# The low half of the feed-forward weights: a negated copy on ScalarE and an adding transfer instead of a VectorE subtraction

## The chip, the core and the metric

The kernel runs on one core of a Trainium2 chip, alone. The metric is the time of one execution on the device in microseconds (us), as the median of its runs. The engines are named as in the profile: PE is TensorE (matmul), PEld its weight load, DVE is VectorE, ACT is ScalarE, POOL is GpSimd, SP is SyncE. SPq, ACTq and POOLq stand for the instruction queues of those engines when they only issue transfers or wait.

## The reference, cut to what matters

One inference step of a two-layer decoder on 512 prompt tokens and 8 sample tokens, model width 1024. Layer one mixes tokens with sliding-window attention, layer two with gated linear attention (GLA). Each is followed by the same gated feed-forward block, and each sublayer by a LayerNorm. The change touches only the weights of the feed-forward block:

```python
D_MODEL = 1024; D_FF = 2816; CONV_W = 3; DEPTH = 2

def conv_ffn(x, buf, w_up, conv_w, conv_b, w_down):
    T = x.shape[1]
    h = x @ w_up                              # (T, 2 * D_FF)
    a, u = h[..., :D_FF], h[..., D_FF:]       # gate, value
    ap = jnp.concatenate([buf.astype(a.dtype), a], axis=1)
    c = conv_b + sum(conv_w[j] * ap[:, j:j + T] for j in range(CONV_W))
    y = (jax.nn.gelu(c, approximate=False) * u) @ w_down
    return y, ap[:, T:]

for i in range(DEPTH):
    ...
    xp = layer_norm(ALPHA * xp + mp, ln_mix_g[i], ln_mix_b[i])
    fp, cp = conv_ffn(xp, buf0, ffn_w_up[i], ffn_conv_w[i], ffn_conv_b[i], ffn_w_down[i])
    xp = layer_norm(ALPHA * xp + fp, ln_ffn_g[i], ln_ffn_b[i])
```

All data are float32.

## The kernel before, in words

**Products in two parts.** The matmuls run in float32r, a shorter format. Each operand is split into a high part (the value rounded to float32r) and a low part (the value minus its high part, also stored as float32r). A product is the sum of three matmuls: high weight by high activation, high weight by low activation, low weight by high activation. In the profile the tiles of the weights are `raw` (the float32 weights as loaded), `wh` (high) and `wl` (low).

**Units.** All weights are cut into 187 units of 128 output features. A unit is a tile of 128 partitions by 1024 elements (512 KB); the first part of a down-projection has units of 128 by 768 (384 KB). Units 0 to 9 are the attention projections, 10 to 17 its output projection, 18 to 85 the feed-forward block of layer one, 86 to 110 GLA, 111 to 118 its output projection, 119 to 186 the feed-forward block of layer two. A feed-forward block has 44 units of the up-projection (gate and value in turn, `ffn_gate` and `ffn_value`) and 24 of the down-projection (`ffn_down`), in three parts: after 6, 14 and 22 pairs of gate and value comes a run of eight down units.

**Two groups of tokens.** Each unit is used twice: by group a (256 prompt tokens) and later by group b (256 prompt tokens and the 8 samples). `order` (line 996 on) writes the PE order of the blocks: block (a, u) is followed by block (b, u minus the lead). The lead is `max(LAG, min(top, p0 + 2 * top - u))`: 5 for the first units of a phase, 4 from the seventh unit on. So in the middle of a feed-forward block the order is (a, u), (b, u - 4), (a, u + 1), (b, u - 3) and so on.

**Buffers of the weights.** `raw` has 2 buffers. `wh` and `wl` have 6 slots, and during a feed-forward block one more (`wx`, the extra slot). A slot is free when group b has used its unit. `run` calls `next_unit` after each b block, and that issues the next load; with seven slots the unit loaded after (b, u) is u + 7. The extra slot is not refilled in the last eight units before the end of each feed-forward block; after that the unit loaded after (b, u) is u + 6. This holds for the last six units of each block, 80 to 85 and 181 to 186.

**Loading a unit** (`load_unit`, line 152 on). SP issues the transfer from DRAM into `raw` (line 162). ACT writes `wh`, a rounding copy (line 167). DVE writes `wl = raw - wh` (line 170). For the few units loaded around the start of a feed-forward block or of GLA (flag `late`) the two steps are traced by `parts` instead (ACT line 181, DVE line 183). Of the 136 feed-forward units 12 are late ones (19 to 24 and 120 to 125).

**Use of a unit.** In most feed-forward blocks group a uses `product2`: for each of the 8 slices of the contraction, one matmul with the high weights over 512 columns (high and low activations side by side, line 221) and one with the low weights over 256 columns (line 222). The low weights are read from the second matmul of the block on. Group b uses `product`: three matmuls for each slice (lines 198, 200 and 202), the third with the low weights. The first four pairs of gate and value and the third part of the down-projection use `product` for group a too.

**What else runs in the feed-forward block.** ACT copies the gate's sums out of PSUM (line 637), scales (642), applies GELU (653) and rounds the product gate times value (228). DVE does the convolution's multiply-adds (643, 644), the product (665) and its low part (229). POOL clears or copies the two columns of history (634, and the copies on line 232). PSUM holds four accumulators.

**Order on each engine.** The kernel is written with the Tile framework, opened with `schedule_with_timeline_sim=True`: the framework takes the instructions in the order in which the program traces them as priorities, and places each on its engine's queue when its own simulation has it ready. So an edit can also change the order of instructions around it. Each engine runs its queue in order.

Of the kernel before, what the change touches and what calls it, by code (L numbers as in the profile page):

```python
# [11 lines left out]
F32 = mybir.dt.float32  # L12
F32R = mybir.dt.float32r
I32 = mybir.dt.int32
AF = mybir.ActivationFunctionType
ALU = mybir.AluOpType
# [81 lines left out]
class Net:  # L98
# [53 lines left out]
    def load_unit(self, u, pieces=1, extra=False, late=False):  # L152
        src, nt = self.units[u][0], self.units[u][1]
        nc = self.nc
        if nt == 0:
            return self.load_rank(u)
        r = self.raw.tile([P, KD * P], F32, name="raw")
        pool = self.wx if extra else self.wts
        h, l = (pool.tile([P, KD * P], F32R, name=name) for name in ("wh", "wl"))
        n = nt * P // pieces  # L160
        for c in (slice(i * n, (i + 1) * n) for i in range(pieces)):
            nc.sync.dma_start(out=r[:, c], in_=src[:, c])
            if late:
                self.spawn(self.parts(u, h[:, c], l[:, c], r[:, c]), 1)
                continue
            if u >= HIACT:
                nc.scalar.activation(h[:, c], r[:, c], AF.Copy)  # L167
            else:
                nc.gpsimd.tensor_scalar(h[:, c], r[:, c], 1.0, 0.0, op0=ALU.mult, op1=ALU.add)
            nc.vector.tensor_tensor(l[:, c], r[:, c], h[:, c].bitcast(F32), op=ALU.subtract)  # L170
        self.w[u] = (h, l)

# [1000 lines left out]
```

## Time and profile before

| | |
|---|---|
| median of 2 runs | 1133.96 us (1133.62 to 1134.3) |
| span of the profiled execution, first to last instruction | 1131.7 us |
| PE busy | 1104.2 us, 98% |
| DVE, ACT, POOL busy | 777.2 us (69%), 565.7 us (50%), 319.3 us (28%) |
| moved by the transfers | 122.81 MB, 109 GB/s over the span |
| feed-forward block of layer one, about | 160 to 520 us of the span |
| feed-forward block of layer two, about | 770 to 1107 us of the span |

The profiled execution is one execution taken by the hardware profiler; of its own time only the span is known, 2.3 us less than the median of the runs. The page's parts are: busy time of each engine, the span in 40 slices, the transfer queues, the chain of work that ended last, groups of instructions, and transfers. A row of a group names line, engine, operation, the tile written and the tiles read, partitions by elements, the count, the busy time, the mean duration in ns, and the idle time of the engine just before, with what ended it. In a timeline each row is: start, duration, engine, line, operation, tiles, and in brackets the idle time before it and what released it. Matmuls overlap: the next starts before the last one's shown end, so the step from start to start is what a matmul costs.

### The profile page before, as it was taken

What the parts mean: (1) busy time and instruction counts of PE and PEld (TensorE: products, weight loads), DVE (VectorE), ACT (ScalarE), POOL (GpSimd) and SP (SyncE); (2) the same over time, 40 slices, a digit from 0 to 9 for tenths busy, and PEclk for the clock granted to TensorE, in tenths of its full rate; (3) what the DMA queues carried; (4) which work ended last, traced back from release to release, by engine and by line L of the source; (5) the groups of instructions that cost most, each with busy time, mean ns of one, the idle gap of its engine ahead of it and who ended that gap; (6) DMA issues with size and microseconds to landing.
All of it is one profiled execution on the core that took longest, in us unless ns stands there. A gap on an engine that the chain in (4) does not pass through costs nothing.

```text
span 1131.7 us, 22912 instructions
## 1 busy us (share of the span) xinstructions
PE 1104.2 (98%) x8806; PEld 1055.1 (93%) x8806; DVE 777.2 (69%) x1626; ACT 565.7 (50%) x1251; POOL 319.3 (28%) x591
## 2 busy tenths in 40 slices
PE   8999999999999999999999999999999999999996
PEld 7997799999999999999899999899999999999995
DVE  7897579655665566568867778779756665566565
ACT  5677556534553245435455556456524553245433
POOL 4575574400110011255211100374400110001243
PEclk9999999999999999999899999999999999999998
DMA  7553023333233233242124354432333223223222
GB/s 244 150 178 96 16 75 101 105 103 121 94 105 102 93 100 106 75 134 94 57 90 145 122 178 160 139 111 94 113 98 127 94 98 109 93 96 110 76 64 76
DMA packets 53804, 122.81 MB, mean 109 GB/s; under 512 B 6808, under 2 KB 27328, under 8 KB 53696
## 3 DMA queue, kind: packets, MB, share of 16 engines
q1 hardware_dynamic: 51536, 119.47, 32.8%
q10 hardware_dynamic: 2160, 1.89, 0.5%
q8 instruction: 69, 1.13, 0.4%
q14 instruction: 39, 0.32, 0.1%
HBM read 108.67 MB, written 8.47 MB: 104 GB/s over the span
## 4 chain that ended last, share of the span: by engine, by line
PE 77%; DVE 10%; DMA 5%; ACT 3%; issue 2%; POOL 1%; SPq 0%; ACTq 0%; DVEq 0%; POOLq 0%
PE accp L198 16%; PE accp L200 16%; PE accp L202 16%; PE accp L221 15%; PE accp L222 8%; DMA vb<-dv 2%; DVE xs_a L355 1%; DVE wl L183 1%; DVE wl L170 1%; DMA raw<-in_w_up 1%; DMA qs<-hl 1%; DVE sgla L910 1%; DVE x_a L353 1%; PE pv L554 1%; ACT pr L523 1%
## 5 line engine op out<-in xcount | busy, mean ns | idle before, releaser
L170 DVE TENSOR_TENSOR wl<-raw,wh 128x1024 fp32r<-128x1024 f32 (+2 forms) x172 | 207.0, 1205 | 103.3 <-ACT wh L167 102.7
L198 PE MATMUL accp<-xh_b,wh 128*128 128x264 f32 x976 | 272.5, 279 | 1.8 <-ACT xh_b L354 1.7
L167 ACT ACTIVATE wh<-raw 128x1024 fp32r<-128x1024 f32 (+2 forms) x168 | 173.6, 1033 | 199.8 <-PE accp L200 187.3
L202 PE MATMUL accp<-xh_b,wl 128*128 128x264 f32 x976 | 270.8, 277 | 0.0
L200 PE MATMUL accp<-xl_b,wh 128*128 128x264 f32 x960 | 266.5, 278 | 0.0
L221 PE MATMUL accp<-xs_a,wh 128*128 128x512 f32 x576 | 196.3, 382 | 0.0
L198 PEld LDWEIGHTS accp<-xh_b,wh 128*128 128x128 f32 x976 | 184.8, 189 | 3.3 <-ACT xh_b L354 2.3
L202 PEld LDWEIGHTS accp<-xh_b,wl 128*128 128x128 f32 x976 | 184.5, 189 | 0.8 <-issue 0.6
L200 PEld LDWEIGHTS accp<-xl_b,wh 128*128 128x128 f32 x960 | 181.6, 189 | 2.5 <-issue 0.4
L222 PE MATMUL accp<-xs_a,wl 128*128 128x256 f32 x576 | 145.4, 273 | 0.0
L198 PE MATMUL accp<-hh_b,wh 128*128 128x264 f32 x480 | 134.2, 280 | 1.7 <-ACT hh_b L228 1.1
L200 PE MATMUL accp<-hl_b,wh 128*128 128x264 f32 x480 | 134.6, 280 | 0.3 <-DVE hl_b L594 0.2
L202 PE MATMUL accp<-hh_b,wl 128*128 128x264 f32 x480 | 133.6, 278 | 0.0
L221 PEld LDWEIGHTS accp<-xs_a,wh 128*128 128x128 f32 x576 | 109.1, 189 | 11.4
L222 PEld LDWEIGHTS accp<-xs_a,wl 128*128 128x128 f32 x576 | 110.2, 191 | 1.9
L198 PE MATMUL accp<-xs_a,wh 128*128 128x256 f32 x400 | 107.6, 284 | 1.4 <-ACT wh L167 0.6
L200 PE MATMUL accp<-xs_a,wh 128*128 128x256 f32 x384 | 103.0, 282 | 0.6 <-DVE xs_a L229 0.3
L198 PEld LDWEIGHTS accp<-hh_b,wh 128*128 128x128 f32 x480 | 91.6, 191 | 2.3 <-ACT hh_b L228 1.6
L200 PEld LDWEIGHTS accp<-hl_b,wh 128*128 128x128 f32 x480 | 91.5, 191 | 1.8 <-DVE hl_b L594 0.4
L202 PEld LDWEIGHTS accp<-hh_b,wl 128*128 128x128 f32 x480 | 91.5, 191 | 0.2
L232 POOL COPY hist<-aext 128x2 f32<-128x2 f32 x44 | 10.2, 231 | 283.7 <-DVE aext L641 277.2
L198 PEld LDWEIGHTS accp<-xs_a,wh 128*128 128x128 f32 x400 | 77.2, 194 | 2.8 <-ACT wh L167 1.0
(338 smaller groups left out, 2505.5 us busy)
## 6 DMA issues: line engine op xcount, KB each, us to landing
raw<-in_w_up SPq DMA_DIRECT2D x88, 512.0 KB, 3.4
raw<-in_w_down SPq DMA_DIRECT2D x32, 512.0 KB, 3.4
raw<-in_w_gla SPq DMA_DIRECT2D x24, 512.0 KB, 3.4
raw<-in_w_mix_o SPq DMA_DIRECT2D x16, 512.0 KB, 4.1
raw<-in_w_down SPq DMA_DIRECT2D x16, 384.0 KB, 3.0
qs<-hl SPq DMA_DIRECT2D x64, 64.0 KB, 2.2
sgla<-in_state_gla SPq DMA_DIRECT2D x16, 256.0 KB, 2.7
vb<-dv SPq DMA_DIRECT2D x16, 256.0 KB, 3.7
```

What stands on the lines that cost most here:

```text
L167: nc.scalar.activation(h[:, c], r[:, c], AF.Copy)
L170: nc.vector.tensor_tensor(l[:, c], r[:, c], h[:, c].bitcast(F32), op=ALU.subtract)
L183: self.nc.vector.tensor_tensor(l, r, h.bitcast(F32), op=ALU.subtract)
L198: nc.tensor.matmul(o, h[:, ks], xh, start=k == 0, stop=False)
L200: nc.tensor.matmul(o, h[:, ks], xl, start=False, stop=False)
L202: nc.tensor.matmul(o, l[:, ks], xh, start=False, stop=not tail and k == nt - 1)
L221: both = lambda: nc.tensor.matmul(o, h[:, ks], in_turn(rs[:, k].rearrange("p t q j -> p t (q j)")), start=k == 0, stop=last)
L222: low = lambda: nc.tensor.matmul(o[:, :P], l[:, ks], in_turn(rh[:, k]), start=False, stop=False)
L353: v = nc.vector.scalar_tensor_tensor(x[:, m], x[:, m], sc(m), rp, op0=ALU.mult, op1=ALU.mult)
L355: xl = nc.vector.scalar_tensor_tensor(g.xl[:, m], parted(x[:, m]), bi(m), g.xh[:, m].bitcast(F32), op0=ALU.add, op1=ALU.subtract)
L523: nc.scalar.activation(pr[:, b, 0:P + 1], sc[:, b, 0:P + 1], AF.Exp, bias=nm[:, b:b + 1], accum_out=den[:, b:b + 1])
L554: mm = nc.tensor.matmul(pv[64 * v:64 * v + 64, b * P:(b + 1) * P], self.vtok[:, kb, 64 * v:64 * v + 64], parts[v][w][:, b], start=i == 0, ...
```

## The change

For feed-forward units that are not late ones, DVE's subtraction is taken out. In its place ACT reads `wh` again and writes its negative into `wl`, and POOL issues a transfer that adds float32 weights onto `wl` where it lies in SBUF. In layer one (`first`: the unit's first argument is the layer) the transfer reads the weights a second time from DRAM. In layer two it reads them from `raw` in SBUF.

```diff
             if u >= HIACT:
                 nc.scalar.activation(h[:, c], r[:, c], AF.Copy)
             else:
                 nc.gpsimd.tensor_scalar(h[:, c], r[:, c], 1.0, 0.0, op0=ALU.mult, op1=ALU.add)
+            if self.units[u][2] in (self.ffn_gate, self.ffn_value, self.ffn_down):
+                first = self.units[u][3][0] == 0
+                nc.scalar.activation(l[:, c], h[:, c].bitcast(F32), AF.Copy, scale=-1.0)
+                nc.gpsimd.dma_start(out=l[:, c], in_=src[:, c] if first else r[:, c], accum_op=ALU.add)
+                continue
             nc.vector.tensor_tensor(l[:, c], r[:, c], h[:, c].bitcast(F32), op=ALU.subtract)
         self.w[u] = (h, l)
```

The `late` branch stands above these lines and ends with its own `continue`, so the late units keep DVE's subtraction, as do the units of attention, GLA and the output projections. The first unit of each feed-forward block (18 and 119) is loaded in the phase before and takes the new lines.

## The prediction

> **What bounds the kernel now.** I read the page first, then the stages, PE's waits, and a timeline from the middle of layer one's feed-forward block.
>
> ```profile
> span 1131.7 us, 22912 instructions
> ...
> PE 1104.2 (98%) x8806; PEld 1055.1 (93%) x8806; DVE 777.2 (69%) x1626; ACT 565.7 (50%) x1251; POOL 319.3 (28%) x591
> ...
> q1 hardware_dynamic: 51536, 119.47, 32.8%
> ...
> raw<-in_w_up SPq DMA_DIRECT2D x88, 512.0 KB, 3.4
> ```
>
> Two stages, one inside each feed-forward block (columns: stage, its length, busy time and instructions of PE, PEld, DVE, ACT, POOL, granted clock, transfer share, GB/s), and the stage at the end:
>
> ```profile
> 300.00:500.00 200.00, 200.00 (x1550) 193.27 (x1549) 119.36 (x220) 88.09 (x160) 29.28 (x83) 1.00 0.31 104
> 786.00:930.00 144.00, 144.00 (x1100) 138.72 (x1099) 93.11 (x175) 68.98 (x128) 24.65 (x71) 1.00 0.33 107
> ...
> 1100.00:1132.00 32.00, 21.25 (x174) 20.38 (x173) 18.38 (x39) 12.59 (x27) 12.77 (x19) 0.88 0.20 67
> ```
>
> What PE waits for that the change touches (total us, times, longest):
>
> ```profile
> PE accp L198 <- ACT wh L167: 0.6, 2, 0.5
> ...
> PE accp L202 <- DVE wl L170: 0.6, 1, 0.6
> ```
>
> PE is the bound: in the feed-forward blocks it never idles, and its idle time in the whole span is 1131.7 - 1104.2 = 27.5 us, a good part of it at the end. DVE's subtraction costs PE 0.6 us in all. So taking it away can gain next to nothing; the question is whether the new, longer way to `wl` stays hidden behind PE.
>
> **The cover there is today.** The timeline, cut to the rows that time one slot:
>
> ```profile
> 404.18 0.28 PE L202 MATMUL accp<-hh_b,wl 128*128 128x264 f32 x1
> 404.43 1.06 ACT L167 ACTIVATE wh<-raw 128x1024 fp32r<-128x1024 f32 x1 [0.83 <-PE accp L200]
> 405.52 1.23 DVE L170 TENSOR_TENSOR wl<-raw,wh 128x1024 fp32r<-128x1024 f32 x1 [0.60 <-ACT wh L167]
> 406.78 0.33 SPq L162 DMA_DIRECT2D raw<-in_w_up  x1
> 409.70 1.06 ACT L167 ACTIVATE wh<-raw 128x1024 fp32r<-128x1024 f32 x1 [1.05 <-PE accp L200]
> 409.83 0.27 PE L222 MATMUL accp<-xs_a,wl 128*128 128x256 f32 x1
> 415.02 1.06 ACT L167 ACTIVATE wh<-raw 128x1024 fp32r<-128x1024 f32 x1 [0.68 <-PE accp L200]
> 415.15 0.27 PE L222 MATMUL accp<-xs_a,wl 128*128 128x256 f32 x1
> ```
>
> At 404.18 group b's block (b, u) ends. That frees a slot, and ACT, which had waited for it, starts the copy for unit u + 7 at 404.43. The period of one unit is 415.15 - 409.83 = 5.32 us. With seven slots and a lead of 4 the PE order after (b, u) is (a, u + 5), (b, u + 1), (a, u + 6), (b, u + 2), (a, u + 7). So the new slot's low part is first read two periods on, at 415.15: 10.72 us after ACT's start. Today it is written at 405.52 + 1.23 = 406.75, which leaves 8.4 us of slack.
>
> The same rows show a second ring. SP's load at 406.78 follows the end of the subtraction by 0.03 us: `raw` has two buffers, and it is the subtraction that frees one.
>
> The last six units of each block have one slot fewer. In layer two they show as ACT's copies after a period without one:
>
> ```profile
> 1057.63 1.06 ACT L167 ACTIVATE wh<-raw 128x1024 fp32r<-128x1024 f32 x1 [1.05 <-PE accp L200]
> 1068.33 1.06 ACT L167 ACTIVATE wh<-raw 128x1024 fp32r<-128x1024 f32 x1 [4.29 <-PE accp L200]
> ...
> 1096.11 1.07 ACT L167 ACTIVATE wh<-raw 128x1024 fp32r<-128x1024 f32 x1 [0.26 <-PE accp L200]
> ```
>
> For those the time to the first low matmul is one period less: 10.72 - 5.32 = 5.4 us.
>
> **The change part by part.** Of 136 feed-forward units 12 are late ones and stay, so 124 change, 62 in each layer, 8 of each 62 with 768 columns.
>
> ```profile
> L170 DVE TENSOR_TENSOR wl<-raw,wh 128x1024 fp32r<-128x1024 f32 x150 | 187.7, 1252 | 90.0 <-ACT wh L167 89.5 <-PE accp L202 0.3
> L170 DVE TENSOR_TENSOR wl<-raw,wh 128x768 fp32r<-128x768 f32 x16 | 15.3, 958 | 13.2 <-ACT wh L167 13.2
> ...
> L167 ACT ACTIVATE wh<-raw 128x1024 fp32r<-128x1024 f32 x150 | 158.8, 1059 | 169.2 <-PE accp L200 157.1 <-DMA raw<-in_w_mix_o 7.5 <-DMA raw<-in_w_up 1.5
> L167 ACT ACTIVATE wh<-raw 128x768 fp32r<-128x768 f32 x16 | 13.5, 846 | 30.1 <-PE accp L200 30.1
> ```
>
> *Removed.* DVE: 108 x 1.252 + 16 x 0.958 = 151 us. By PE's waits worth 0.6 us at most; I take 0.
>
> *ACT, the negation.* The same size as the copy before it: 108 x 1.06 + 16 x 0.85 = 128 us. Per unit ACT goes from 68.98 / 144 x 5.32 = 2.5 to 3.6 us of 5.32, so it fits. Behind it stand the copies that empty PSUM, at most 1.06 us later; four accumulators cover that (two blocks are 5.32 us). Cost 0 beside its part in the chain below. Without that cover each block would lose up to 1 us.
>
> *POOL, the issue.* POOL is busy 24.65 of 144 us here. Behind the issue in its queue stand the tiny history copies:
>
> ```profile
> L232 POOL COPY nconv_p<-aext 128x2 f32<-128x2 f32 x44 | 29.9, 679 | 118.3 <-ACT aext L637 118.2
> L232 POOL COPY hist<-aext 128x2 f32<-128x2 f32 x44 | 10.2, 231 | 283.7 <-DVE aext L641 277.2 <-ACT aext L637 6.6
> ```
>
> They feed the next convolution, not PE, and have idle time ahead of them: cost 0. If the issue is queued behind such a copy instead, it waits for DVE, some 1.5 us; that belongs to the range.
>
> *The adding transfer.* No transfer on POOL's queue and no adding one is in this trace. Let X be the time from the end of the negation until `wl` is readable. The nearest row is the plain 512 KB load, from issue to landing (least, median, most):
>
> ```profile
> DMA to landing us min/median/max: 2.8/3.4/5.9
> ```
>
> Lower bound: a plain load, 3.4 us. Upper bound: two of the slowest ones in sequence, as the transfer reads two operands, 11.8 us. In between: a load's share of the 16 transfer engines is 0.328 x 1131.7 / 119.47 x 0.524 = 1.63 us. A second read costs between that and a whole load, so about 2.5 us. POOL's issue I estimate at 1.0 us against SP's 0.33 (its copy of two columns already takes 0.68), so 0.7 more. X = 3.4 + 2.5 + 0.7 = 6.6 us, nearer to the lower bound since the pieces of one transfer overlap.
>
> The Trainium skill, Collectives: The Full Stack, section "The bandwidth ceiling: the fold count and why AG ≠ RS ≠ AR", says that adding in a transfer costs through its two source reads, both on one ring, and not through the addition. By that the second read would be 1.63 us, X 5.7 and the sum below about 1168. No run here shows it yet.
>
> *The chain.* From ACT's start: 1.06 + 1.06 + about 0.1 of handovers + X = 2.2 + X. What it may take:
> - Layer one, seven slots: 10.72, so X up to 8.5. `raw` is free earlier than today, after the copy. Cost at X = 6.6: 0.
> - Layer two: the transfer reads `raw`, so the buffer is held until it has landed. One turn of a `raw` buffer is 2.2 + X + 0.1 + 3.4 (the next load) = 5.7 + X, and serves every second unit: it must be below 2 x 5.32 = 10.64, so X below 4.9. At 6.6 the turn is 12.3 and each unit loses (12.3 - 10.64) / 2 = 0.83 us. PE's slack of 8.5 - 6.6 = 1.9 us is used up first. Units 126 to 180 are 55: 55 x 0.83 - 1.9 = 44 us. What is late next is ACT's copy (it will wait for the load and not for PE), then PE at the first low matmul.
> - The last six units of each layer: 5.4, so X up to 3.2. At 6.6 the chain is 3.4 us late; a b block follows its a block directly, so the delay comes once in two units: 1.7 x 6 x 2 layers = 20 us.
>
> Sum: 0 + 44 + 20 = 64 us. The profiled execution becomes 1131.7 + 64 = 1195.7; the runs' median lies 1133.96 - 1131.7 = 2.3 above the span, so 1198 us, 5.6% slower.
>
> **The rivals.**
> *Fast enough (not slower).* If X stays under 4.9, the `raw` ring never closes and only the two ends pay. At X = 4.4: (4.4 - 3.2) / 2 x 12 = 7 us, 1141 us. The sum passes 2%, 22.7 us, at X about 5.4. For it: the plain load lands in 3.4, and in layer two nothing is read from DRAM. Against it: two reads, and an issue in software. It is also what the Trainium skill makes of it: DMA: Bandwidth & Descriptors, section "Anatomy of one DMA — SWDGE (gpsimd) path", gives 2.0 us plus bytes / 436 GB/s; with the second read counted again that is 4.4 us. No transfer of this trace runs that path.
>
> *Layer one falls too (slower still).* Each period now holds a load of 1.63 us on the transfer engines; two more reads make 4.9 of 5.32 us, 92%, so loads and adding transfers queue for each other. At X = 10: layer one, whose ring closes over three units, (10 - 8.5) / 3 x 55 = 28; layer two (10 - 4.9) / 2 x 55 = 140; ends (10 - 3.2) / 2 x 12 = 41; 209 in all, 1343 us. For it: the 92%, and the 5.9 us landing of today. Against it: the share is worked out for reads that cost as much as a whole load does now.
>
> *Faster.* DVE's relief would have to win back PE's idle time; all of it is 27.5 us, 1106 us. Against it: PE waits 0.6 us for this subtraction.
>
> *The order moves.* The framework may order the engines' queues anew. With group b's block put ahead of a late a block the ends' 20 us vanish, but the `raw` ring stays: 1178 us. And if gaps on PE lower the clock (0.88 in the last stage, where PE is busy 21 of 32 us), layer two's steps grow by some per cent. Both lie inside the range.
>
> **How the numbers follow.** Forecast, with X between 5.4 and 8.5: 0.51, moved order included. Fast enough: 0.24. Layer one falls too: 0.23. Faster: 0.02. Two per cent is about what a measurement here tells from no change. So faster 0.02, same 0.24, slower 0.74. The range goes from 1137 (X at the plain load's 3.4, the two ends almost free) to 1340 (X near 10); the two tails beyond hold about 0.2.
>
> **What would show it.** The raw loads of layer two should land just ahead of ACT's copies, and ACT's wait of line 167 should turn from PE to the load there, while in layer one it stays PE. The copies' spacing should be 5.32 us in layer one, about 6.15 in layer two, about 7 in the last six units of each. DVE's busy time falls by about 151 us, ACT's rises by about 128. Wrong if layer one's spacing grows too (X over 8.5), or if layer two keeps 5.32 (X under 4.9), or if PE waits for ACT's other copies or for POOL's history.

## The result, and the profile after

The changed kernel takes 1231.51 us (median; 1229.92 to 1233.11) against 1133.96: ratio 1.086, 95% interval 1.083 to 1.090. It is 97.6 us slower. The forecast was 1198, in a range of 1137 to 1340. One of the five executions of the last experiment below, the profiled one, was slower as a whole (1232.3 us at a granted clock of 0.976, the others 1209.5 to 1215.4 us at 0.981 to 0.985), and its time is left out there.

The page after, the lines that answer to those of before; `q0` is POOL's own transfer queue:

```profile
span 1228.2 us, 23160 instructions
...
PE 1130.6 (92%) x8806; PEld 1064.5 (87%) x8806; DVE 644.9 (53%) x1502; ACT 671.5 (55%) x1375; POOL 388.2 (32%) x715
...
q1 hardware_dynamic: 51536, 119.47, 29.8%
q0 software_dynamic: 17856, 62.92, 29.2%
...
raw<-in_w_up SPq DMA_DIRECT2D x88, 512.0 KB, 4.3
wl<-raw POOLq DMA_DIRECT2D x54, 512.0 KB, 5.1
wl<-in_w_up POOLq DMA_DIRECT2D x38, 512.0 KB, 6.5
```

DVE's busy time fell by 132 us and ACT's rose by 106. 124 adding transfers move 62.92 MB more. The span grew by 96.5 us: PE's idle time rose by 70.1 us, from 27.5 to 97.6, and its busy time by 26.4 us for the same 8806 matmuls (their shown ends overlap, so this split is rough). Two stages show in which layer (same columns as before the change):

```profile
207.00:480.00 273.00, 272.00 (x2047) 260.55 (x2046) 108.64 (x250) 165.26 (x267) 65.92 (x156) 1.00 0.87 195
785.00:1130.00 345.00, 293.74 (x2097) 272.44 (x2095) 117.25 (x276) 171.45 (x288) 75.35 (x167) 0.98 0.65 154
```

In layer one PE is nearly as full as before (1 us idle of 273), although the transfer engines are busier there (0.87) than in layer two (0.65), where PE lacks 51 us. What PE and ACT wait for now (total us, times, longest):

```profile
ACT wh L167 <- PE accp L205: 99.3, 70, 4.4
ACT wh L167 <- DMA raw<-in_w_up: 94.7, 24, 7.1
...
ACT wh L167 <- DMA raw<-in_w_down: 63.2, 14, 7.8
```

```profile
PE accp L227 <- DMA wl<-raw: 44.2, 29, 4.6
PE accp L207 <- DMA wl<-raw: 8.8, 8, 2.7
PE accp L207 <- DMA wl<-in_w_down: 4.8, 3, 1.8
...
PE accp L207 <- DMA wl<-in_w_up: 2.1, 1, 2.1
```

PE waits for low parts that were added from `raw` (layer two), hardly for those from DRAM (layer one). And ACT's copy, which before waited for a slot that PE frees, now also waits for the raw load, 158 us in all. Layer one's steady state:

```profile
410.12 1.06 ACT L167 ACTIVATE wh<-raw 128x1024 fp32r<-128x1024 f32 x1 [0.83 <-PE accp L205]
411.21 1.06 ACT L172 ACTIVATE wl<-wh 128x1024 fp32r<-128x1024 f32 x1
412.56 0.86 POOL L173 DMA_DIRECT2D wl<-in_w_up  x1 [4.30 <-ACT wl L172]
415.44 1.06 ACT L167 ACTIVATE wh<-raw 128x1024 fp32r<-128x1024 f32 x1 [1.07 <-PE accp L205]
420.76 1.06 ACT L167 ACTIVATE wh<-raw 128x1024 fp32r<-128x1024 f32 x1 [0.63 <-PE accp L205]
```

The copies are 5.32 us apart, as before. One turn of a `raw` buffer in layer two, in the order of time:

```profile
1072.59 0.86 POOL L173 DMA_DIRECT2D wl<-raw  x1 [2.82 <-ACT aext L642]
1073.41 0.33 SPq L162 DMA_DIRECT2D raw<-in_w_up  x1
1078.62 0.33 SPq L162 DMA_DIRECT2D raw<-in_w_up  x1
1079.27 1.06 ACT L167 ACTIVATE wh<-raw 128x1024 fp32r<-128x1024 f32 x1 [5.62 <-DMA raw<-in_w_up]
1080.23 0.40 ACT L658 ACTIVATE conv<-conv 128x256 f32<-128x256 f32 x1
1080.54 0.36 ACT L642 COPY aext<-accp 128x264 f32<-128x264 f32 x1
1080.80 0.57 ACT L647 ACTIVATE conv<-accp,par 128x256 f32<-128x256 f32 x1
1081.26 1.05 ACT L172 ACTIVATE wl<-wh 128x1024 fp32r<-128x1024 f32 x1
1082.60 0.86 POOL L173 DMA_DIRECT2D wl<-raw  x1 [1.33 <-ACT hprod L667]
1087.05 0.38 PE L227 MATMUL accp<-xs_a,wl 128*128 128x256 f32 x1 [2.45 <-DMA wl<-raw]
1087.06 0.33 SPq L162 DMA_DIRECT2D raw<-in_w_up  x1
```

Load at 1073.41, copy at 1079.27, negation at 1081.26, transfer issued at 1082.60. At 1087.05 it has landed: PE, which had waited for it, starts, and 0.01 us later SP issues the next load into the same buffer. The turn is 13.65 us for two units. It is one of the longer turns; the mean is worked out further down. The loads at 1073.41 and 1078.62 belong to the two buffers; the first of them runs beside the other buffer's adding transfer, issued at 1072.59.

### The profile page after: what moved, and what is told of

It reads as the page before. It is cut to its first block, busy times and chain, and to the rows that moved or that the text cites. A ratio compares the mean times of both kernels' runs of the same rounds, so it can differ in the third digit from the quotient of the medians.

```text
span 1228.2 us, 23160 instructions
## 1 busy us (share of the span) xinstructions
PE 1130.6 (92%) x8806; PEld 1064.5 (87%) x8806; DVE 644.9 (53%) x1502; ACT 671.5 (55%) x1375; POOL 388.2 (32%) x715
## 3 DMA queue, kind: packets, MB, share of 16 engines
q0 software_dynamic: 17856, 62.92, 29.2%
## 4 chain that ended last, share of the span: by engine, by line
PE 39%; DMA 27%; DVE 12%; ACT 9%; issue 9%; POOL 3%; SPq 1%; POOLq 0%; DVEq 0%; ACTq 0%
DMA wl<-raw 11%; PE accp L207 8%; PE accp L205 8%; PE accp L203 8%; PE accp L226 7%; DMA raw<-in_w_up 6%; PE accp L227 3%; DMA raw<-in_w_down 3%; ACT wl L172 2%; ACT wh L167 2%; DMA vb<-dv 2%; DMA wl<-in_w_down 1%; DMA wl<-in_w_up 1%; DVE wl L175 1%; DVE xs_a L360 1%
## 5 line engine op out<-in xcount | busy, mean ns | idle before, releaser
L226 PE MATMUL accp<-xs_a,wh 128*128 128x512 f32 x576 | 201.8, 387 | 0.0
L227 PE MATMUL accp<-xs_a,wl 128*128 128x256 f32 x576 | 150.3, 281 | 36.8 <-DMA wl<-raw 35.8
L172 ACT ACTIVATE wl<-wh 128x1024 fp32r<-128x1024 f32 (+1 forms) x124 | 126.8, 1023 | 1.0
L226 PEld LDWEIGHTS accp<-xs_a,wh 128*128 128x128 f32 x576 | 111.0, 193 | 11.2
L173 POOL DMA_DIRECT2D wl<-raw x62 | 53.8, 867 | 187.8 <-ACT aext L642 64.9
L207 PE MATMUL accp<-hs_a,wl 128*128 128x256 f32 x256 | 71.1, 281 | 11.0 <-DMA wl<-raw 6.1
```

Source lines behind the costliest of these rows:

```text
L172: nc.scalar.activation(l[:, c], h[:, c].bitcast(F32), AF.Copy, scale=-1.0)
L173: nc.gpsimd.dma_start(out=l[:, c], in_=src[:, c] if first else r[:, c], accum_op=ALU.add)
L207: nc.tensor.matmul(o, l[:, ks], xh, start=False, stop=not tail and k == nt - 1)
L226: both = lambda: nc.tensor.matmul(o, h[:, ks], in_turn(rs[:, k].rearrange("p t q j -> p t (q j)")), start=k == 0, stop=last)
L227: low = lambda: nc.tensor.matmul(o[:, :P], l[:, ks], in_turn(rh[:, k]), start=False, stop=False)
```

## The experiments

Theory R: layer two loses because `raw` is held until the transfer that reads it has landed, so that the turn of two buffers sets the pace; beside it only units with less cover lose. Theory E: the adding transfers' length and the crowding of the transfer engines cost the time. Theory A: ACT's extra work does. Runs with one time each are set against the run of the kernel before on the same chip: 1137.12 us in the first four experiments, where twelve other times of that kernel run from 1132.06 to 1137.42.

**Both layers from DRAM.**

```diff
-                nc.gpsimd.dma_start(out=l[:, c], in_=src[:, c] if first else r[:, c], accum_op=ALU.add)
+                nc.gpsimd.dma_start(out=l[:, c], in_=src[:, c], accum_op=ALU.add)
```

> The changed kernel with layer two's adding transfer reading DRAM too, so that the raw buffer is free after ACT's copy in both layers. Theory R (layer two loses because raw is held until the transfer that reads it has landed): layer two behaves like layer one, steady copies 5.32 us apart, some 12 to 15 us lost at its ends, about 1160 us (1150 to 1175). Theory E (what costs is the length of the adding transfers and the crowding of the transfer engines): transfers from DRAM took 6.5 against 5.1 us from SBUF, so layer two gets slower by about 0.7 us a unit, about 1270 us. Theory A (ACT's extra work and its queue's order cost the time): unchanged, 1231 us.

1168.95 us, beside 1137.12 before: 31.8 us lost where the changed kernel lost 97.6. ACT's copies hardly wait for loads any more; the waits of this kernel's line 167:

```profile
ACT wh L167 <- PE accp L205: 163.9, 119, 4.4
ACT wh L167 <- DMA raw<-in_w_mix_o: 8.8, 4, 4.1
```

Reading 512 KB more from DRAM for each unit of layer two saves two thirds of the loss. R stands; E and A, which wanted 1270 and 1231, do not.

**Both layers from SBUF.**

```diff
-                nc.gpsimd.dma_start(out=l[:, c], in_=src[:, c] if first else r[:, c], accum_op=ALU.add)
+                nc.gpsimd.dma_start(out=l[:, c], in_=r[:, c], accum_op=ALU.add)
```

> The changed kernel with layer one's adding transfer reading raw in SBUF too. Theory R: layer one now loses as layer two does, 1.3 to 1.4 us a unit over some 55 units, about 1304 us (1285 to 1325), copies of both layers in pairs 13 to 14 us apart. Theory E: transfers from SBUF are shorter and load less, so layer one keeps 5.32 us and the time stays at 1231 us or below. Theory A: 1231 us.

1310.81 us beside 1137.12: 173.7 lost. Layer one now loses as layer two does; PE's wait is twice that of the changed kernel:

```profile
PE accp L227 <- DMA wl<-raw: 95.5, 60, 3.5
```

So it is the source of the transfer and not the layer.

**A third raw buffer in layer two.**

```diff
+        if layer:
+            self.rx, self.rx_cm = self.open("raw1", 3)
...
-        r = self.raw.tile([P, KD * P], F32, name="raw")
+        r = (self.rx or self.raw).tile([P, KD * P], F32, name="raw")
```

> The changed kernel with a pool of three raw buffers of its own in layer two's feed-forward block (two before). Transfers, sources and ACT's work as in the changed kernel. Theory R: a turn of 13.7 us over three buffers allows 4.6 us a unit, below PE's 5.32, so layer two's steady loss goes, about 1160 us (1145 to 1180). Theory E and theory A: the same transfers and the same ACT work, about 1231 us.

1166.63 us beside 1137.12: 29.5 lost. Same transfers, same source, same ACT work as in the changed kernel, and the adding transfers even land later (5.9 us against 5.1); one more buffer takes 68 of 97.6 us away. This is the plainest evidence for R.

**Negation kept, transfer out.**

```diff
                 nc.scalar.activation(l[:, c], h[:, c].bitcast(F32), AF.Copy, scale=-1.0)
-                nc.gpsimd.dma_start(out=l[:, c], in_=src[:, c] if first else r[:, c], accum_op=ALU.add)
-                continue
             nc.vector.tensor_tensor(l[:, c], r[:, c], h[:, c].bitcast(F32), op=ALU.subtract)
```

> The changed kernel with ACT's negation kept and the transfer taken out: DVE subtracts as before, over what ACT wrote. The result is the full one. Theory R and theory E: no transfer, nothing lost beyond ACT's 1.06 us in the chain, 1134 us (1131 to 1139). Theory A: most of the 97 us stays, 1190 us or more.

1136.05 us beside 1137.12. ACT's 127 us of extra work alone cost nothing that shows.

**What remains: the ends.** Three kernels with both layers from DRAM, in which only some units take the new way; the edit is one condition:

```diff
-            if self.units[u][2] in (self.ffn_gate, self.ffn_value, self.ffn_down):
+            if 40 <= u < 80 or 141 <= u < 181:                            # middle
+            if 80 <= u < 86 or 181 <= u:                                  # last six
+            if u == 18 or 25 <= u < 40 or u == 119 or 126 <= u < 141:     # first units
```

> Negation and adding transfer (from DRAM in both layers) only for units 40 to 79 and 141 to 180, the stretch with seven slots and the regular order; all others keep DVE's subtraction. 80 of 124 units still take the new way. Theory R (only the held raw buffer and the units with less cover cost time): nothing is lost, within 3 us of before. Theory E (the adding transfers themselves or their crowding cost PE something everywhere): at least a third of what was lost with both layers on DRAM (32 us), so 10 us or more above before.

1136.80 against 1133.85, ratio 1.002 (1.0005 to 1.0035): 3.0 us by the medians for 80 adding transfers, a little above noise. PE's matmuls with the low parts wait 0.8 us for them in all:

```profile
L227 PE MATMUL accp<-xs_a,wl 128*128 128x256 f32 x576 | 145.7, 273 | 0.8 <-DMA wl<-in_w_up 0.8
```

In the middle the new way is hidden, as R says.

> Negation and adding transfer (from DRAM) only for the last six units of each layer, 80 to 85 and 181 to 186, which have one slot less. Theory R with the transfer as measured (6.2 us, plus 0.3 from ACT to POOL): a chain of 8.7 us against a cover of 5.4, 1.6 us a unit, 12 units: 16 to 22 us above before. Rival: PE's order and the LayerNorm behind these units absorb it, under 6 us.

1149.32, ratio 1.0136 (1.0119 to 1.0153): 15.5 us, just under what R gave. PE's wait for the low parts in that kernel, and the landing of the transfers:

```profile
PE accp L207 <- DMA wl<-in_w_down: 8.1, 6, 3.0
...
wl<-in_w_down POOLq DMA_DIRECT2D x12, 512.0 KB, 7.9
```

PE waits six times for the 12 units. But these waits add up to 8.1 us only, although the transfers took 7.9 us and not the 6.2 that R reckoned with. Where the other 7.4 us lie stays open, so the total fits R better than its parts do.

> Negation and adding transfer (from DRAM) only for units 18, 25 to 39, 119 and 126 to 140: the start of each feed-forward block, where the lead is 5 for six units and the first down units have only six slices (a period of about 4.1 us). The prediction charged nothing here. Theory R, widened to these units: the cover there is one period or two short ones, 5 to 9 us, against a chain of 8.7, some 8 to 16 us above before. The prediction as it stood: 0 to 3 us.

1154.47, ratio 1.0183 (1.0168 to 1.0199): 20.6 us, more than either side expected.

```profile
PE accp L207 <- DMA wl<-in_w_up: 5.5, 2, 3.6
PE accp L227 <- DMA wl<-in_w_up: 3.1, 4, 1.5
```

PE's direct waits for low parts are 8.6 us of it, all for units of the up-projection (`in_w_up`); for the down units with their short period there is none. The loss lies where the two feed-forward blocks begin (before, then this kernel; same columns as above):

```profile
143.00:207.00 64.00, 62.98 (x538) 61.78 (x537) 52.87 (x99) 37.54 (x73) 36.10 (x53) 1.00 0.31 100
760.00:830.00 70.00, 68.65 (x550) 66.25 (x549) 56.31 (x108) 38.57 (x77) 29.24 (x53) 1.00 0.32 103
```

```profile
143.00:207.00 64.00, 60.64 (x520) 59.22 (x519) 47.12 (x92) 40.78 (x77) 36.55 (x55) 1.00 0.43 121
760.00:830.00 70.00, 62.84 (x484) 60.23 (x483) 46.39 (x93) 42.52 (x79) 31.55 (x60) 0.95 0.53 131
```

From 760 to 830 us PE is busy 5.8 us less, and the granted clock there is 0.95 in place of 1.00. At the end of layer one, from 480 to 560 us, nothing is lost (77.1 us busy, 77.2 before). What makes up the 12 us beside the direct waits stays open.

The three parts give 3.0 + 15.5 + 20.6 = 39 us, and all units together from DRAM lost 31.8: the parts don't simply add up.

**A plain copy for the adding transfer.**

```diff
-                nc.gpsimd.dma_start(out=l[:, c], in_=src[:, c] if first else r[:, c], accum_op=ALU.add)
+                nc.gpsimd.dma_start(out=l[:, c], in_=src[:, c] if first else r[:, c])
```

> The changed kernel with the transfer on POOL's queue copying the weights over wl and not adding them; left out is the addition, so wl holds the weights and not their low part. Same sources, bytes written and waits, one read less. If the second read costs time (my 2.5 us for it): the transfer lands after about 3 to 4 us where the adding one took 5.1 from SBUF and 6.2 to 6.5 from DRAM, the raw turn of layer two falls by 1.5 to 2 us, about 1185 us (1165 to 1205). Rival: the software path, not the addition, makes it slow; landing and time as in the changed kernel, about 1231 us.

1157.58 us beside 1133.85, below the range that was expected. The transfers of this kernel:

```profile
q0 software_dynamic: 17856, 62.92, 16.9%
...
raw<-in_w_up SPq DMA_DIRECT2D x88, 512.0 KB, 3.4
wl<-raw POOLq DMA_DIRECT2D x54, 512.0 KB, 3.6
wl<-in_w_up POOLq DMA_DIRECT2D x38, 512.0 KB, 4.3
```

The addition, with the second read that it needs, costs 5.1 - 3.6 = 1.5 us from SBUF and 6.5 - 4.3 = 2.2 from DRAM until landing. It also costs the loads beside it: without it their median goes back from 4.3 to the 3.4 of before. Both are in the raw turn, and the time is 74 us shorter. The run takes out the read and the addition together and can't tell one from the other.

**The raw turn by itself.**

```diff
-            if self.units[u][2] in (self.ffn_gate, self.ffn_value, self.ffn_down):
+            if 141 <= u < 181:
```

> Negation and adding transfer only for units 141 to 180, the middle of layer two, reading raw in SBUF with its two buffers; all other units keep DVE's subtraction. Theory R by itself: the turn of a raw buffer measured in the changed kernel, some 13.2 to 13.7 us for two units against 10.64, 1.3 to 1.5 us a unit, less some 3 us of slack: 40 units, 48 to 58 us above before, 1182 to 1192 us. As the prediction sized the turn (12.3 us): 40 x 0.83 - 2 = 31 us, 1165 us. With the middle from DRAM the same stretch of both layers cost 2 us.

1187.02 against 1134.17, ratio 1.0478 (1.0450 to 1.0506): 52.9 us for 40 units, 1.32 us each. That is what the turn as measured gave; the turn as the prediction sized it gave 31 us.

**The negation on DVE.**

```diff
-                nc.scalar.activation(l[:, c], h[:, c].bitcast(F32), AF.Copy, scale=-1.0)
+                nc.vector.tensor_scalar(l[:, c], h[:, c].bitcast(F32), -1.0, None, op0=ALU.mult)
```

> The changed kernel with the negation on DVE and not on ACT; transfers and sources as there. In the changed kernel every second negation stands behind three of ACT's copies, 0.9 us after the high part is done. If that is part of the raw turn (theory R with ACT's queue in the turn): the turn loses 0.5 to 1 us, about 14 to 28 us off, 1203 to 1218 us. If only transfer and load set the turn: 1231 us, or a few us more since DVE's negation waits for ACT's copy across engines.

1213.0 us beside 1134.17, 18.5 us below the changed kernel and inside what ACT's queue in the turn was to give. But the variant also makes the negation itself shorter, 0.71 us on DVE against 1.05 on ACT (its row here, then that of the changed kernel):

```profile
L172 DVE TENSOR_SCALAR wl<-wh 128x1024 fp32r<-128x1024 f32 x108 | 76.5, 709 | 203.1 <-ACT wh L167 203.0
L172 ACT ACTIVATE wl<-wh 128x1024 fp32r<-128x1024 f32 x108 | 113.4, 1050 | 0.9
```

By an estimate from these rows the 0.34 us, once in each turn of two units, are worth 0.17 x 55 = 9 us, about half of the gain. So the negation's place in ACT's queue can account for the other half; this run does not separate the two. ACT's work as such cost nothing (the fourth experiment).

None of these beats the kernel before. None could by much: PE's idle time there is 27.5 us, and in the blocks that the change touches it has none.

## Why the prediction was right, and where it was off

**Right: PE is the bound and DVE's relief is worth nothing.** DVE is 132 us lighter and nothing got faster; in the middle-only kernel, where the new way is hidden, DVE is 88 us lighter (689.6 against 777.2) and the time is 3.0 us above before. The forecast of 151 us less on DVE and 128 more on ACT came out as 132 and 106: the negations are 126.8 us by their rows, but an engine's busy time counts overlapping instructions once (in the turn above line 642 begins before line 658 ends).

**Right: layer one's cover.** The chain there is 412.56 - 410.12 = 2.4 us to the issue and 6.5 to the landing, 8.9 of the 10.72 us allowed. The copies kept 5.32 us.

**Right: the raw ring, and what is late next.** The text said that ACT's copy would wait for the load in place of PE, then PE at the first low matmul of group a. That is what the waits show, and the third buffer and the change of source bear it out.

**Off by size: the turn, 12.3 us forecast, 13.65 in the turn shown and 13.2 on average.** By its terms:

| term | forecast | measured in the turn above |
|---|---|---|
| load, issue to copy | 3.5 | 1079.27 - 1073.41 = 5.86 |
| copy | 1.06 | 1.06 |
| wait of the negation in ACT's queue | 0 | 1081.26 - 1080.33 = 0.93 |
| negation | 1.06 | 1.05 |
| from its end to the landing (X) and handovers | 6.7 | 1087.06 - 1082.31 = 4.75 |

X was too high for SBUF: by the median it is 0.29 us to the issue and 5.1 to the landing, 5.4 and not 6.6 (4.75 in this turn). The issue estimate of 1.0 us was near (0.87); the second read costs 1.5 and not 2.5. But X and the load were priced one by one from rows where each ran alone. In the ring they meet: one buffer's load runs beside the other's adding transfer. The transfer issued at 1072.59 needs 6.03 us (to SP's next load at 1078.62), that of 1082.60 only 4.45, and the load beside the first one 5.86. The prediction had the crowding, but only as a rival for layer one. The Trainium skill, DMA: Bandwidth & Descriptors, section "Issuing engines are not separate DMA queues", says that transfers from different engines share the same 16 transfer engines and interleave; the 5.86 against 3.4 fits.

The other missed term is the order in ACT's queue. The text counted the copies that stand behind the negation, and took 0; here three of ACT's instructions (lines 658, 642 and 647) stand ahead of it. In the turn shown they cost 0.93 us, on a ring that had become the bound; over all units of layer two that read `raw` the mean is 0.4. Up to about half of the DVE variant's 18.5 us can be put down to it.

The forecast came as near as it did partly by luck: X was too high and the load and the queue were too low. With X at 5.4 and the rest of the sum unchanged the loss comes to (11.1 - 10.64) / 2 x 55 - 3.1 + (5.4 - 3.2) / 2 x 12 = 23 us, a time of 1157 us.

What a unit lost is read from ACT's copies. Units 126, 145 and 179 before (unit 180 at 1057.63 stands in the prediction), then 126, 145, 179 and 180 in the changed kernel:

```profile
788.74 1.05 ACT L167 ACTIVATE wh<-raw 128x1024 fp32r<-128x1024 f32 x1
871.48 1.06 ACT L167 ACTIVATE wh<-raw 128x1024 fp32r<-128x1024 f32 x1
1052.31 1.06 ACT L167 ACTIVATE wh<-raw 128x1024 fp32r<-128x1024 f32 x1 [0.69 <-PE accp L200]
```

```profile
802.87 1.05 ACT L167 ACTIVATE wh<-raw 128x1024 fp32r<-128x1024 f32 x1
914.97 1.06 ACT L167 ACTIVATE wh<-raw 128x1024 fp32r<-128x1024 f32 x1 [2.74 <-DMA raw<-in_w_up]
1139.83 1.04 ACT L167 ACTIVATE wh<-raw 128x1024 fp32r<-128x1024 f32 x1
1147.84 1.06 ACT L167 ACTIVATE wh<-raw 128x1024 fp32r<-128x1024 f32 x1 [4.29 <-DMA raw<-in_w_down]
```

From unit 145 to 179 the copies were 180.83 / 34 = 5.32 us apart and are now 224.86 / 34 = 6.61: a mean turn of 13.2 us, and 1.29 us lost on each unit where 0.83 was forecast. From 126 to 145, with the eight short down units, they were 4.35 us apart and not 5.32, and are now 5.90: 1.55 us lost on each. So units 126 to 180 lose (1147.84 - 1057.63) - (802.87 - 788.74) = 76 us and not 44. That is nearly all of the 33 us by which the forecast fell short. The other 20 us of the span's growth lie outside these units, 14 ahead of them and 6 behind. The forecast also had 20 us there, but all of it in the last six units of the two layers; as the first units of layer one cost something too, that match is partly luck.

**The second read.** From the shares, an adding transfer takes 0.292 x 1228.2 / 124 = 2.9 us of the 16 engines, a plain one 0.169 x 1155.9 / 124 = 1.6: adding costs 1.3 more, somewhat less than the plain transfer itself. The landing shows 1.5 for SBUF; the forecast's 2.5 was too careful. The Trainium skill, Collectives: The Full Stack, section "The bandwidth ceiling: the fold count and why AG ≠ RS ≠ AR", lays the cost of adding in a transfer to this second read; the 1.3 fits, though no run here has the read without the addition. The X of 5.7 that the text worked out from that rule was nearer to the measured 5.4 than its own 6.6, and the time that went with it, 1168 us, was farther off.

**The last six units: 20 us forecast, 15.5 measured** in the kernel that has only these (from DRAM). PE waits once in two units, as the text said, but 1.4 us each time (8.1 / 6) and not 3.4; the rest of the 15.5 us is not explained by these waits.

**Missed: the first units.** The text put their cost at 0 in layer one and at the steady price in layer two. In the kernel that has only these units they cost 20.6 us, of which 8.6 are direct waits. The lead of 5 does not explain it by itself: of the first six units of a block, which have that lead, only the first takes the new way, as the next ones are late units. Why the cover is short for the units behind them stays open, as said.

**The rivals.** "Fast enough" wanted X below 4.9 and worked with 4.4; from SBUF the median was 5.4 (4.75 in the turn above), and the load beside it had grown from 3.4 to 5.86 us there. "Layer one falls too" wanted X above 8.5 and got 0.29 + 6.5 = 6.8, with transfer engines 87% busy against the 92% that it reckoned with. "The order moves" is not settled: whether blocks changed places, and what that cost, no run takes by itself. The granted clock in layer two's stage was 0.98, where it had been 1.00.

## What to carry to other kernels

A new reader of a buffer moves the time at which it is free. So before a step is handed to a slower path, follow each buffer that the step reads to its next filling, and add up the whole turn, not only the way to the consumer. Price the terms of such a turn as they run there: transfers beside each other, instructions behind what their engine has queued. Where a second copy of the data can be fetched from elsewhere (DRAM here), or one more buffer fits, the turn opens: 66 to 68 of 97.6 us.

## What the runs showed of the hardware that was not expected

Adding onto SBUF from SBUF landed 1.4 us sooner than from DRAM (5.1 against 6.5 us for 512 KB; 5.0 and 6.2 in the kernels with one source for both layers); without the addition the difference was 0.7 (3.6 against 4.3). POOL's own time for an issue was 0.87 us with the addition and 0.54 without (the changed kernel, then the plain copy):

```profile
L173 POOL DMA_DIRECT2D wl<-raw x62 | 53.8, 867 | 187.8 <-ACT aext L642 64.9 <-ACT wl L172 62.9 <-ACT hprod L667 35.8
```

```profile
L173 POOL DMA_DIRECT2D wl<-raw x62 | 33.4, 539 | 171.9 <-ACT aext L642 68.7 <-ACT wl L172 55.7 <-ACT hprod L667 25.7
```

From the end of ACT's negation to POOL's issue 0.29 us pass (411.21 + 1.06 = 412.27 to 412.56) even with POOL idle, against 0.03 from ACT's copy to DVE's subtraction before the change. And transfer engines that were 87% busy, as in layer one, did not slow PE down as long as the cover was there.
